# Value tiles of two strided attention groups: computed in token order and sorted by residue through DRAM

## Chip, cores, metric

One core of a Trainium2 chip runs the kernel. The metric is the device time of one launch in microseconds (us), the median of several runs. The engines are TensorE (PE in the profile; PEld is its weight load), VectorE (DVE), ScalarE (ACT), GpSimd (POOL) and SyncE (SP), which issues DMAs.

## What is computed

One layer of a decoder trunk: 512 tokens, width 1024, float32. One projection gives queries, keys and values of three token mixers and three gates; their outputs are gated, merged, projected and normalised, and a squared-ReLU MLP follows. The change touches the third mixer, a dilated window attention with three groups of four heads of 128 columns:

```python
DIL_PAIRS = ((128, 1), (512, 4), (2048, 16))   # window, dilation of group 0, 1, 2

def dilated_group(q, k, v, bias_table, window, dilation):
    # Query t reads t, t-d, ..., t-window.
    def to_strided(a):
        a = jnp.pad(a, ((0, 0), (0, Lp * dilation - S), (0, 0), (0, 0)))
        a = a.reshape(B, Lp, dilation, H, dh).transpose(0, 2, 3, 1, 4)
        return a.reshape(B, dilation, H, nb, n, dh)
    ...
    o = jnp.einsum('brhcqk,brhckd->brhcqd', prob.astype(vb.dtype), vb)
```

In groups 1 and 2 a query reads only keys of its own residue (token number modulo 4, or modulo 16). The kernel keeps both groups sorted by residue modulo 4: tile c holds the 128 tokens c, c+4, c+8, ...

## The kernel before

Every matmul operand is split into a high and a low part of the type that TensorE reads in one pass (`xh`, `xl` for the input, `h`, `l` for weights), and a product is three matmuls: high by high, high by low, low by high.

The work is a list of items. An item of kind "T" computes 128 columns of the projection, transposed (`mm3`, L87 to L89); kind "V" computes values, 128 tokens by 512 columns in each of four items (`v_items`, L331 to L333). An item of 24 matmuls goes into one of two PSUM banks and is copied out by ACT or DVE in turn (`cp`, L96 and L98; for values the copy makes the tile `V[name, g, tt]`). Weights come by SP's queue (`raw`, L182), and ACT and DVE split them (`wh`, L212; `wl`, L214) into a ring of seven chunks.

The main loop walks the items in the order of `main_order` and calls `step()` once before each item and once in its middle. A step resumes the attention generators that are active (`sb_head`, `dil_head`, `da_block`) and those in `pending`; what they issue falls between matmuls of the items. So the list of items and the number of steps set the order on each engine.

`dil_head` computes the scores of one head for the three groups, normalises them (L1540, L1544), transposes them on TensorE (L1556 for group 0, L1565 for groups 1 and 2), steps on until all values are there, and multiplies them by the value tiles (L1577 for group 0, L1582 for 1 and 2), with `po[:, c::4]` putting the columns of residue c back in token order. The wait for the values is a test while the program is written, not on the chip:

```python
while any(("dl_v", g, 3) not in V for g in range(3)):
    yield
po = at_bank()
```

The values of group g stand in the list after the second head's queries and keys of that group. For g > 0 their items read the input with a stride of four tokens (`xh[k][:, tt::4]`) as the stationary operand, so each tile comes out holding one residue.

POOL's queue carries sums of weight tiles for later stages: `gsum`, `usum`, `dsum`, copied from DRAM to DRAM (L804) and accumulated (L802) in pieces of 512 KB. Each is tied to a weight split on DVE, which spreads them over the main stream. POOL issues its DMAs in program order. The attention tiles live in 42 buffers of one pool (`slot`); a tile takes over a buffer when the last user of the tile before has finished.

Of the kernel before, what the change touches and what calls it, by code (L numbers as in the profile page):

```python
# [10 lines left out]
F32 = mybir.dt.float32  # L11
# [5 lines left out]
S = 512  # L17
D = 1024
P = 128
# [36 lines left out]
def trunk(tc, a, out):  # L56
    nc = tc.nc
    es = ExitStack()
    with es:
# [4 lines left out]
        dram = es.enter_context(tc.tile_pool(name="dram", bufs=1, space=bass.MemoryType.DRAM))  # L64
# [5 lines left out]
        def nm(s):  # L70
            uid[0] += 1
            return f"{s}_{uid[0]}"

        def slot(name, dt=F32):
            return big.tile([P, 512], dt, name=nm(name), tag="s", bufs=NSLOT)
# [7 lines left out]
        def at_bank():  # L83
            return psum.tile([P, 512], F32, name=nm("at"), tag="at", bufs=6)
# [8 lines left out]
        def cp(o, i):  # L93
            flip[0] ^= 1
            if flip[0]:
                nc.scalar.copy(o, i)  # L96
            else:
                nc.vector.tensor_copy(o, i)  # L98
# [53 lines left out]
        def chunk(src, w):  # L152
            return chunk_of(load(src, w))
# [78 lines left out]
        def item(cs, mm, ev, need=None, bank=None, size=1.0):  # L232
            items.append({"c": cs, "mm": mm, "ev": ev, "need": need, "bank": bank, "size": size})
# [9 lines left out]
        xh = [xhT[:, k, :] for k in range(8)]  # L243
        xl = [xlT[:, k, :] for k in range(8)]
# [7 lines left out]
        V = {}  # L252
# [42 lines left out]
        def first_item():  # L295
# [21 lines left out]
                    t_evac(*order[t][1:])(ps[t])  # L317
            item([cs[k][0] for k in (0, 1, 3, 5, 7)], mm, ev, bank=lambda: (at_bank(), at_bank()))

        def v_items(nv, name, g):  # L320
            cs = [chunk(a["wv"][nv, c].rearrange("p k n -> p (k n)"), 1024) for c in range(4)]
            for tt in range(4):
                def mm(ps, tt=tt):
                    for k in range(8):
                        c = cs[k // 2]
                        s = slice((k % 2) * 512, (k % 2) * 512 + 512)
                        if name == "dl_v" and g > 0:
                            x1, x2 = xh[k][:, tt::4], xl[k][:, tt::4]
                        else:
                            x1, x2 = xh[k][:, tt * P:tt * P + P], xl[k][:, tt * P:tt * P + P]  # L330
                        nc.tensor.matmul(ps, x1, c["h"][:, s], start=k == 0, stop=False)  # L331
                        nc.tensor.matmul(ps, x1, c["l"][:, s], start=False, stop=False)  # L332
                        nc.tensor.matmul(ps, x2, c["h"][:, s], start=False, stop=k == 7)  # L333
                        if k == 3:
                            yield

                def ev(ps, tt=tt):
                    if name == "sb_v":
                        v = [slot(name, F32R).rearrange("p (h two d) -> p h two d", two=2, d=64) for _ in range(2)]
                        pv = ps.rearrange("p (h d) -> p h d", d=64)  # L340
                        for i in range(2):
                            hs = slice(4 * i, 4 * i + 4)
                            nc.scalar.copy(v[i][:, :, 0, :], pv[:, hs, :])
                            nc.vector.tensor_sub(v[i][:, :, 1, :], pv[:, hs, :], v[i][:, :, 0, :].bitcast(F32))
                        V[name, g, tt] = v
                    else:
                        t = slot(name)
                        cp(t, ps)
                        V[name, g, tt] = t
                item(cs if tt == 3 else [], mm, ev, need=cs)  # L350

        nt, nv = 2, 0
# [2 lines left out]
        for kind, name, j in order[2:]:  # L355
            if kind == "T":
                if name == "gate":
                    continue
                t_item(nt, name, j)
                nt += 1  # L360
            else:
                v_items(nv, name, j)
                nv += 1
# [200 lines left out]
        x1 = {}  # L564
# [1026 lines left out]
        pending = []  # L1591
# [232 lines left out]
```

## Time and profile before

| | us |
|---|---|
| median of 3 runs (1065.19 to 1065.71) | 1065.29 |
| the profiled execution, own time | 1065.43 |
| its span, first to last instruction | 1063.7 |
| TensorE busy | 1051.9 |
| VectorE busy | 750.8 |
| ScalarE busy | 558.5 |
| GpSimd busy | 129.6 |

The profile is of one execution. The groups of its page name an instruction by line, engine, operation, and tiles as out<-in. Matmuls overlap, so the start of one to the start of the next, not the duration, is what one costs. The values of group 0 are computed between 142 and 169 us, of group 1 between 185 and 213, of group 2 between 226 and 259; the first two heads' products with the values lie between 266 and 274.

### The profile page before, as it was taken

The numbers are of one execution on the slowest core, as the hardware profiler recorded it, in microseconds if no ns is written. First come the engines' busy times: TensorE is split into PE (matmuls) and PEld (weight loads), VectorE is DVE, ScalarE is ACT, GpSimd is POOL, SyncE is SP. The second block draws the span as 40 slices with busy tenths as digits, with TensorE's granted clock in tenths as the row PEclk, the third lists the DMA queues.
The fourth block names the chain that finished last, engine by engine and source line by source line (L and its number), as shares of the span: only waits on it lengthen the run. The fifth ranks groups of instructions, "written<-read, shape, count | busy, mean of one in ns | idle before, by whom it ended". The sixth has DMA issues, their size and how long they took to land.

```text
span 1063.7 us, 15533 instructions
## 1 busy us (share of the span) xinstructions
PE 1051.9 (99%) x5826; PEld 913.4 (86%) x5826; DVE 750.8 (71%) x1345; ACT 558.5 (53%) x975; POOL 129.6 (12%) x200
## 2 busy tenths in 40 slices
PE   9999999999999999999999999999999999999996
PEld 6887788999888888888999988888999989989885
DVE  6888667547353757768767774888677877877965
ACT  7665545425232546447545452685765665665741
POOL 0000402021121102230111030101100010000000
PEclk9999999999999999999999999999999999999999
DMA  8333756393896819783766583149989788867602
GB/s 316 131 130 100 222 135 175 122 304 84 285 242 200 230 40 315 146 251 98 195 185 191 185 285 139 61 145 273 264 279 275 241 238 258 256 226 245 187 17 79
DMA packets 59452, 206.11 MB, mean 194 GB/s; under 512 B 7433, under 2 KB 8345, under 8 KB 59377
## 3 DMA queue, kind: packets, MB, share of 16 engines
q1 hardware_dynamic: 36192, 123.66, 33.4%
q0 software_dynamic: 22608, 80.55, 29.4%
q8 instruction: 45, 0.74, 0.3%
q10 hardware_dynamic: 576, 0.92, 0.2%
q14 instruction: 31, 0.25, 0.1%
HBM read 202.97 MB, written 73.42 MB: 260 GB/s over the span
## 4 chain that ended last, share of the span: by engine, by line
PE 89%; DVE 7%; issue 2%; ACT 2%; DMA 0%; POOL 0%; SPq 0%; DVEq 0%; POOLq 0%
PE mm L87 13%; PE mm L89 13%; PE mm L88 13%; PE at L87 4%; PE at L962 4%; PE at L963 4%; PE at L964 4%; PE at L89 4%; PE at L88 4%; PE mm L331 3%; PE mm L333 3%; PE mm L332 3%; DVE wl L214 2%; PE at L131 1%; PE at L312 1%
## 5 line engine op out<-in xcount | busy, mean ns | idle before, releaser
L212 ACT CAST wh<-raw 128x1024 fp32r<-128x1024 f32 (+1 forms) x243 | 250.7, 1035 | 254.6 <-PE mm L88 149.5
L214 DVE TENSOR_TENSOR wl<-raw,wh 128x1024 fp32r<-128x1024 f32 (+1 forms) x243 | 291.6, 1205 | 110.4 <-ACT wh L212 106.9
L87 PE MATMUL mm<-xhT,wh 128*128 128x512 f32 x368 | 146.8, 399 | 0.0
L89 PE MATMUL mm<-xhT,wl 128*128 128x512 f32 x368 | 144.5, 393 | 0.0
L88 PE MATMUL mm<-xlT,wh 128*128 128x512 f32 x368 | 144.1, 392 | 0.0
L89 PEld LDWEIGHTS mm<-xhT,wl 128*128 128x128 f32 x368 | 69.1, 188 | 15.0 <-DVE wl L214 0.3
L87 PEld LDWEIGHTS mm<-xhT,wh 128*128 128x128 f32 x368 | 69.2, 188 | 13.7 <-issue 0.4
L88 PEld LDWEIGHTS mm<-xlT,wh 128*128 128x128 f32 x368 | 69.2, 188 | 13.0
L962 PE MATMUL at<-wh,hh 128*128 128x512 f32 x188 | 73.7, 392 | 0.0
L963 PE MATMUL at<-wl,hh 128*128 128x512 f32 x188 | 73.7, 392 | 0.0
L87 PE MATMUL mm<-x1hT,wh 128*128 128x256 f32 x256 | 73.7, 288 | 0.0
L964 PE MATMUL at<-wh,hl 128*128 128x512 f32 x188 | 73.1, 389 | 0.0
L88 PE MATMUL mm<-x1lT,wh 128*128 128x256 f32 x256 | 72.3, 283 | 0.0
L89 PE MATMUL mm<-x1hT,wl 128*128 128x256 f32 x256 | 71.9, 283 | 0.0
L331 PE MATMUL mm<-wh,xhT 128*128 128x512 f32 x160 | 64.6, 404 | 0.0
L333 PE MATMUL mm<-wh,xlT 128*128 128x512 f32 x160 | 63.1, 394 | 0.0
L332 PE MATMUL mm<-wl,xhT 128*128 128x512 f32 x160 | 62.9, 393 | 0.0
L802 POOL DMA_DIRECT2D usum<-in_wu_dram x32 | 27.6, 862 | 233.5 <-DVE wl L214 222.0
L87 PEld LDWEIGHTS mm<-x1hT,wh 128*128 128x128 f32 x256 | 48.8, 191 | 4.7 <-ACT up L896 2.7
L88 PEld LDWEIGHTS mm<-x1lT,wh 128*128 128x128 f32 x256 | 48.9, 191 | 1.5
L89 PEld LDWEIGHTS mm<-x1hT,wl 128*128 128x128 f32 x256 | 48.6, 191 | 0.0
L802 POOL DMA_DIRECT2D dsum<-in_wd_dram x28 | 26.2, 935 | 133.5 <-DVE wl L214 128.5
(435 smaller groups left out, 2560.5 us busy)
## 6 DMA issues: line engine op xcount, KB each, us to landing
usum<-in_wu_dram POOLq DMA_DIRECT2D x48, 512.0 KB, 7.9
raw<-in_wt_dram SPq DMA_DIRECT2D x46, 512.0 KB, 5.1
dsum<-in_wd_dram POOLq DMA_DIRECT2D x42, 512.0 KB, 9.0
raw<-usum SPq DMA_DIRECT2D x32, 512.0 KB, 5.7
raw<-dsum SPq DMA_DIRECT2D x28, 512.0 KB, 5.0
raw<-in_wd_dram SPq DMA_DIRECT2D x25, 512.0 KB, 4.7
raw<-in_wu_dram SPq DMA_DIRECT2D x24, 512.0 KB, 6.6
raw<-in_wv_dram SPq DMA_DIRECT2D x20, 512.0 KB, 5.6
```

Of the source, the lines that this page charges most:

```text
L87: nc.tensor.matmul(ps, wh, xh, start=start, stop=False, skip_group_check=True)
L88: nc.tensor.matmul(ps, wh, xl, start=False, stop=False, skip_group_check=True)
L89: nc.tensor.matmul(ps, wl, xh, start=False, stop=stop, skip_group_check=True)
L212: i = nc.scalar.copy(h, raw)
L214: i = nc.vector.tensor_sub(lo, raw, h.bitcast(F32))
L331: nc.tensor.matmul(ps, x1, c["h"][:, s], start=k == 0, stop=False)
L332: nc.tensor.matmul(ps, x1, c["l"][:, s], start=False, stop=False)
L333: nc.tensor.matmul(ps, x2, c["h"][:, s], start=False, stop=k == 7)
L802: i = nc.gpsimd.dma_start(o, i, accum_op=OP.add, max_dma_last_dim=4096)
L962: nc.tensor.matmul(ps, h[:, q], c["h"][:, s], start=go, stop=False, skip_group_check=True)
L963: nc.tensor.matmul(ps, h[:, q], c["l"][:, s], start=False, stop=False, skip_group_check=True)
L964: nc.tensor.matmul(ps, lo[:, q], c["h"][:, s], start=False, stop=end, skip_group_check=True)
```

## The change

The values of groups 1 and 2 are computed like those of group 0, from 128 consecutive tokens. Each of the four tiles is stored to a DRAM tensor `vd[g]` after its copy from PSUM. A generator in `pending` passes two steps after the last store, issues four loads, each of every fourth row of `vd[g]`, passes three more steps, and only then enters the loaded tiles as `V["dl_v", g, c]`. Stores and loads are issued by POOL.

```diff
+        vd = {g: dram.tile([S, 512], F32, name=f"vd{g}") for g in (1, 2)}
+
+        def by_residue(g):
+            for _ in range(WRITE):
+                yield
+            ts = []
+            for c in range(4):
+                t = slot("dl_v")
+                nc.gpsimd.dma_start(t, vd[g].rearrange("(n c) d -> c n d", c=4)[c])
+                ts.append(t)
+            for _ in range(READ):
+                yield
+            for c in range(4):
+                V["dl_v", g, c] = ts[c]
+
+        WRITE, READ = 2, 3
+
         def v_items(nv, name, g):
...
-                        if name == "dl_v" and g > 0:
-                            x1, x2 = xh[k][:, tt::4], xl[k][:, tt::4]
-                        else:
-                            x1, x2 = xh[k][:, tt * P:tt * P + P], xl[k][:, tt * P:tt * P + P]
+                        x1, x2 = xh[k][:, tt * P:tt * P + P], xl[k][:, tt * P:tt * P + P]
                         nc.tensor.matmul(ps, x1, c["h"][:, s], start=k == 0, stop=False)
...
                         t = slot(name)
                         cp(t, ps)
-                        V[name, g, tt] = t
+                        if name == "dl_v" and g > 0:
+                            nc.gpsimd.dma_start(vd[g][tt * P:tt * P + P, :], t)
+                            if tt == 3:
+                                pending.append(by_residue(g))
+                        else:
+                            V[name, g, tt] = t
```

## The prediction

> **What bounds the kernel now.** I read the page first: span, busy times, the chain that ended last.
>
> ```profile
> span 1063.7 us, 15533 instructions
> PE 1051.9 (99%) x5826; PEld 913.4 (86%) x5826; DVE 750.8 (71%) x1345; ACT 558.5 (53%) x975; POOL 129.6 (12%) x200
> PE 89%; DVE 7%; issue 2%; ACT 2%; DMA 0%; POOL 0%; SPq 0%; DVEq 0%; POOLq 0%
> ```
>
> TensorE is busy 99% of the span and 89% of the last chain. A microsecond that its stream of matmuls loses or saves anywhere in the middle goes almost whole into the time; DMA and POOL matter only when TensorE has to wait for them.
>
> Next, the view of one source line, L331, whole and then between 184 and 213 us, where group 1 is computed. The figures after the colon are ns, least/median/most.
>
> ```profile
> L331 PEld LDWEIGHTS mm<-wh,xhT x160: 187/188/333, 32.6 to 401.5; 128*128 128x128 f32 x160
> ...
> L331 PEld LDWEIGHTS mm<-wh,xhT x32: 308/310/317, 184.7 to 212.1; 128*128 128x128 f32 x32
> ```
>
> The weight load of a token slice with stride 4 takes 310 ns, the usual one 188. Whether that reaches the matmuls is told by the timeline of TensorE (start, duration in us).
>
> ```profile
> 142.35 0.40 PE L331 MATMUL mm<-wh,xhT 128*128 128x512 f32 x1
> ...
> 151.03 0.40 PE L331 MATMUL mm<-wh,xhT 128*128 128x512 f32 x1
> ...
> 156.29 0.39 PE L333 MATMUL mm<-wh,xlT 128*128 128x512 f32 x1
> ...
> 184.92 0.40 PE L331 MATMUL mm<-wh,xhT 128*128 128x512 f32 x1
> ...
> 190.33 0.39 PE L333 MATMUL mm<-wh,xlT 128*128 128x512 f32 x1
> ...
> 191.27 0.51 PE L331 MATMUL mm<-wh,xhT 128*128 128x512 f32 x1
> ...
> 255.19 0.60 PE L331 MATMUL mm<-wh,xhT 128*128 128x512 f32 x1
> ...
> 274.03 0.47 PE L87 MATMUL mm<-xhT,wh 128*128 128x512 f32 x1
> 274.35 0.40 PE L88 MATMUL mm<-xlT,wh 128*128 128x512 f32 x1
> ...
> 284.36 0.39 PE L87 MATMUL mm<-xhT,wh 128*128 128x512 f32 x1
> ```
>
> **The gain.** 151.03 to 156.29 is one item of group 0 (24 matmuls, 23 steps): 0.2287 us a step. 184.92 to 190.33 is one of group 1: 0.2352. So most of the longer load lies under the matmul before it, and 0.0065 comes through (0.0077 against the 44 steps from 274.35 to 284.36, 0.2275 each). It comes through more where TensorE returns from attention work with short matmuls: the first matmul takes 0.51 instead of 0.40 (191.27 against 142.35, after 256-column matmuls) and 0.60 instead of 0.47 (255.19 against 274.03, after fp32 ones). The two groups have 2 x 4 x 24 = 192 such matmuls. I count ten such returns in the timeline, the first and one of the last of them shown: four of 0.11 to 0.12, one of 0.06, five of 0.125, together about 1.15 us. The other 182 give 182 x 0.0065 to 0.008 = 1.2 to 1.5. Sum: 2.35 to 2.65; I take **2.45 us**, 1.1 of it in group 1 and 1.35 in group 2.
>
> A rule speaks against this: the Trainium skill, "TensorE: Matmul & The Clock Gate", section "LDWEIGHTS (loading the stationary operand)", has the load's time depend on the number of columns alone, about 107 ns for 128, with no word of stride, and its section "Step-by-step: what each phase is for" has it run under the matmul before. By it the gain would be nothing. The trace disagrees: 310 against 188 ns, and 0.2352 against 0.2287 between matmuls.
>
> **What is added.** Per group: four stores of 256 KB (each behind its copy from PSUM) and four loads of 256 KB, all issued by POOL, on the queue of the weight sums. The order of the built program shows the rest: nothing moves on TensorE but the value products of heads 0 and 1 (L1577, L1582). They go from their place after the transposes to a point one and nearly two items later, since the five steps of the generator pass first. ACT and DVE keep their order, but for copies of those products.
>
> ```profile
> 266.63 1.68 PE L1577 MATMUL at<-pt,dl_v 128*128 128x256 f32 x8
> 268.15 1.95 PE L1582 MATMUL at<-pt,dl_v 128*128 128x128 f32 x16
> 269.94 1.04 PE L1565 MATMUL at<-ident,L 128*128 128x128 f32 x8
> 270.81 1.68 PE L1577 MATMUL at<-pt,dl_v 128*128 128x256 f32 x8
> ...
> 266.22 1.13 DVE L1544 TENSOR_SCALAR L<-L,mxx 128x256 f32<-128x256 f32 x4
> ```
>
> The two blocks take 269.94 - 266.63 = 3.31 and 274.03 - 270.81 = 3.22 us; they now stand before the matmul that starts at 284.36. Moving them uncovers the transposes L1565: they come straight after L1556, at 266.63 on the old clock, and need the four scalings L1544, done one after another from 266.22 to 267.35. The third block of columns cannot be transposed before about 267.1, the fourth before 267.35: **+0.4 us**, where the first products hid it before. The blocks now stand alone, one more change between fp32 and the rounded kind (0.32 against 0.23 us to the next matmul): **+0.1**.
>
> **Do the loads arrive in time?** TensorE comes to the products at 284.36 - 6.53 - 2.45 + 0.4 = 275.8. The products with group 0 take 268.15 - 266.63 = 1.52, those with group 1 half of 269.94 - 268.15, 0.9; so the first tile of group 2 is wanted at 278.2 and the fourth, three products of 0.22 later, at 278.8. What stands in POOL's queue then (timeline; below each stretch of it the issues of narrow windows, in the same order, with the us from issue to landing):
>
> ```profile
> 258.03 0.81 POOL L802 DMA_DIRECT2D usum<-in_wu_dram  x1 [23.46 <-DVE wl L214]
> 258.56 1.13 POOL L802 DMA_DIRECT2D dsum<-in_wd_dram  x1
> ...
> 258.79 0.69 DVE L98 COPY dl_v<-mm 128x512 f32<-128x512 f32 x1
> ...
> 262.87 0.52 POOL L804 DMA_DIRECT2D dsum<-in_wd_dram  x1 [0.92 <-DVE sel L1522]
> 269.24 0.52 POOL L804 DMA_DIRECT2D usum<-in_wu_dram  x1 [5.86 <-DVE wl L214]
> 269.75 0.52 POOL L804 DMA_DIRECT2D dsum<-in_wd_dram  x1
> usum<-in_wu_dram POOLq DMA_DIRECT2D x1, 512.0 KB, 6.4
> dsum<-in_wd_dram POOLq DMA_DIRECT2D x1, 512.0 KB, 10.5
> dsum<-in_wd_dram POOLq DMA_DIRECT2D x1, 512.0 KB, 14.5
> usum<-in_wu_dram POOLq DMA_DIRECT2D x1, 512.0 KB, 9.4
> dsum<-in_wd_dram POOLq DMA_DIRECT2D x1, 512.0 KB, 10.1
> ...
> 298.38 2.48 POOL L1187 DMA_DIRECT2D sh<-rv  x4
> sh<-rv POOLq DMA_DIRECT2D x4, 256.0 KB, 9.1
> out_dram<-xn ACTq DMA_DIRECT2D x1, 256.0 KB, 2.0
> ```
>
> The last store of group 2 follows the copy that ends at 259.48, so it is queued behind the two accumulating sums (landed 264.4 and 269.1). Four plain copies of 512 KB follow, the last landing at 262.87 + 14.5 = 277.4. The loads wait for the store, are issued near 268, and stand behind those copies. With the gain the stage is 2.45 earlier: 274.9. Then five pieces of 256 KB are extra, the store and four loads. A piece costs half of what the sums show, 269.1 - 264.4 = 4.7 for 512 KB, so 2.3, as the upper bound; the lower bound is 0, for a store that fits into a gap (alone, one takes 2.0 us from issue to landing, the last row). The two plain copies issued last land at 278.6 and 279.9, 1.2 apart, so 0.6 for 256 KB. The nearest rows in kind are the four table loads of 256 KB, issued in 2.48 us and landing 9.1 (median) after issue, so in queue one behind the other; they bracket nothing tighter. I take 1.0, nearer to the plain copies than to the sums: the fourth load lands at 279.9 and TensorE waits **1.1 us** (0 to 7.6 by the bounds; 274.9 + 5 x 2.3 = 286.4). Everything on TensorE queues behind this wait.
>
> By the Trainium skill, "DMA: Bandwidth & Descriptors", section "Anatomy of one DMA — SWDGE (gpsimd) path", a transfer takes 2.0 us plus its bytes at 436 GB/s, an estimate of 2.6 us for 256 KB; store and loads would be over near 265, and the sum would be the one without this wait. The 14.5 us of the row at 262.87 disagree, because the queue is not empty.
>
> Group 1 has the same hop 40 us before its use; that cover is ample. Its last store has another reader, though: the tile's buffer goes to a later attention tile, so DVE's L1366 now waits for the store's landing.
>
> ```profile
> 213.61 0.96 POOL L802 DMA_DIRECT2D usum<-in_wu_dram  x1
> usum<-in_wu_dram POOLq DMA_DIRECT2D x1, 512.0 KB, 11.9
> ...
> 223.30 0.36 DVE L1366 CAST ah<-a 128x384 fp32r<-128x384 f32 x1 [1.75 <-ACT a L1363]
> ...
> 224.77 0.69 DVE L1367 TENSOR_TENSOR al<-a,ah 128x512 fp32r<-128x512 f32 x1
> ...
> 229.91 0.28 PE L1378 MATMUL at<-al,sb_v 128*64 128x256 f32 x1
> ```
>
> The sum ahead lands at 225.5, the store 0.6 to 2.3 later, both 1.1 earlier in the new run: 225.0 to 226.7. L1366 would have started at 222.2, so DVE stands 2.8 to 4.5 us, with the split, a key copy and a weight split queued behind. The cover is 229.91 - (224.77 + 0.69) = 4.45 us until TensorE reads the result. **0** in the sum; 0.1 at the bound, and whatever the store lands later than 226.7 goes one for one to TensorE. The weight splits behind it feed a ring seven deep. The weight sums that POOL issues a few us later are read in later stages. The view of the waits has POOL standing 222 us for the weight splits that pace them:
>
> ```profile
> POOL usum L802 <- DVE wl L214: 222.0, 25, 36.0
> ```
>
> So a sum that is late by a few us has idle time to catch up in: 0, and SP's loads of the sums would pay if it hadn't.
>
> **Sum.** The profiled execution took 1065.43 us (span 1063.7 and 1.7 around it; the median of the runs is 1065.29). 1065.43 - 2.45 + 0.4 + 0.1 + 1.1 + 0 = **1064.6 us**. A measurement of this kernel can tell about 0.2%, 2.1 us, from no change, so this is a saving inside that bound.
>
> **Rivals.**
> Everything covered: the extra pieces cost 0.6 or less, the fourth load lands by 277.9 and nothing waits. The time is then 1063.5, and 1062.8 if the gain is 2.65 and the transposes do not wait. For it: the 0.6 of the two plain copies. Against: it needs every term at its good end. It passes the 0.2% bound only with both of the last conditions.
>
> Late loads (slower): the mechanism above at the price of the accumulating sums. One load is 2.3 us, the fourth lands at 286.4, TensorE waits 7.6: 1071.1. Past 1.6 us a piece (fourth load at 282.9, a wait of 4.1) the change is slower by over 0.2%. For it: every DMA of this stretch is 6 to 15 us from issue to landing, and the loads need the store first. Against: the pieces are plain ones.
>
> A buffer wait on DVE or ACT: the last store of group 1 lands 4 us later than I work out, near 230. DVE then stands over 7 us and TensorE 4: 1068.6. Against it: a sum of 512 KB is 4.7 us behind the one before, and the store has half its bytes.
>
> No gain: the load is hidden and the change only adds: 1064.6 + 2.45 = 1067.0. The steps of 0.2352 speak against it.
>
> **How the numbers follow.** Forecast (1063.8 to 1067): 0.44. Everything covered: 0.25, of it 0.17 past the bound. Late loads (1067 to 1071): 0.2, of it 0.18 past the bound. DVE: 0.07, nearly all past it. No gain: 0.04, half past it. Faster by over 0.2%: 0.17; slower: 0.18 + 0.07 + 0.02 = 0.27; within: 0.56. The range is 1062.8, the good end of every term, to 1068.5, which leaves the far half of the late loads and part of the DVE case out. The likeliest case's own range is 1063.8 to 1067.
>
> **What would show it.** Right: weight loads of L331's successor all near 188 ns; steps of 0.228 in groups 1 and 2; a wait of 0.5 to 2 us on TensorE before the products with group 2, ended by a load; 0.4 before the transposes. Wrong: no idle time there (covered), more than 4 us there (late loads), idle time near 228 ended by DVE (buffer wait), steps still at 0.235 (no gain).

## The result, and the profile after

The changed kernel takes **1070.72 us** (median of 8 runs, 1067.46 to 1074.38), the kernel before on the same chip 1065.6 (1065.19 to 1066.04): a ratio of 1.0047, 95% interval 1.0035 to 1.006. It is slower by 5 us, and where the runs of before lie within 1 us, those of after lie within 7. The profiled execution is one of the shortest: own time 1067.54, 2.1 over that of before.

The page of after first: span, busy times, the chain that ended last.

```profile
span 1065.8 us, 15575 instructions
PE 1051.2 (99%) x5826; PEld 903.9 (85%) x5826; DVE 750.7 (70%) x1345; ACT 558.5 (52%) x975; POOL 138.5 (13%) x216
PE 83%; DVE 8%; DMA 3%; issue 3%; ACT 2%; POOL 1%; SPq 0%; DVEq 0%; POOLq 0%
```

TensorE is busy 0.7 us less in a span that is 2.1 longer, and DMA, which had no share of the last chain, has 3%. The view of the value line (L346, before L331) and two rows of TensorE's timeline show that the gain itself came:

```profile
L346 PEld LDWEIGHTS mm<-wh,xhT x160: 187/188/200, 32.8 to 402.5; 128*128 128x128 f32 x160
...
185.09 0.39 PE L346 MATMUL mm<-wh,xhT 128*128 128x512 f32 x1
...
190.30 0.40 PE L348 MATMUL mm<-wh,xlT 128*128 128x512 f32 x1
```

No weight load takes 310 ns any more, and an item of group 1 has steps of (190.30 - 185.09) / 23 = 0.2265 us instead of 0.2352. Matched matmul by matmul against before, TensorE gains 1.1 us in group 1 (from 0.2 behind at 184 us to 0.9 ahead at 213) and 1.0 in group 2 (between 229 and 262). The rest is loss. The first loss is near 228, behind the first matmuls of group 2, in the timelines of DVE and TensorE:

```profile
219.40 1.22 DVE L214 TENSOR_TENSOR wl<-raw,wh 128x1024 fp32r<-128x1024 f32 x1 [1.80 <-ACT wh L212]
226.66 0.36 DVE L1386 CAST ah<-a 128x384 fp32r<-128x384 f32 x1 [6.03 <-DMA vd<-dl_v]
...
228.12 0.69 DVE L1387 TENSOR_TENSOR al<-a,ah 128x512 fp32r<-128x512 f32 x1
...
228.87 0.44 PE L1398 MATMUL at<-al,sb_v 128*64 128x512 f32 x1 [0.30 <-DVE al L1387]
```

DVE stands 6.03 us until the last store of group 1 has landed and so freed the buffer. The matmul that reads DVE's last result has 0.30 of idle time before it; by the starts of the matmuls, TensorE loses 0.6 in all here. The second loss is larger: the value products of the first two heads.

```profile
276.62 1.68 PE L1597 MATMUL at<-pt,dl_v 128*128 128x256 f32 x8
278.13 1.48 PE L1602 MATMUL at<-pt,dl_v 128*128 128x128 f32 x10
280.55 0.97 PE L1602 MATMUL at<-pt,dl_v 128*128 128x128 f32 x4 [0.94 <-DMA dl_v<-vd]
281.70 0.49 PE L1602 MATMUL at<-pt,dl_v 128*128 128x128 f32 x2 [0.18 <-DMA dl_v<-vd]
282.03 1.68 PE L1597 MATMUL at<-pt,dl_v 128*128 128x256 f32 x8
283.55 1.95 PE L1602 MATMUL at<-pt,dl_v 128*128 128x128 f32 x16
285.25 0.47 PE L87 MATMUL mm<-xhT,wh 128*128 128x512 f32 x1
```

Undisturbed, the four groups take 6.52 us (the last experiments show it); here 285.25 - 276.62 = 8.63, so 2.1 is lost, and the rows name the loads as what ended the waits. After that, two small things: a wait of 0.34 at 541, and 0.8 at the end of the program, which comes back below.

Two views tell how the DMAs stood: issues with the time to landing, and windows of 5 us. A row of the second has the window, its length, the busy time of PE, PEld, DVE, ACT and POOL (in brackets the number of instructions), the granted clock (1.00 is full speed), the DMA engines' busy share, and the GB/s that they moved.

```profile
dl_v<-vd POOLq DMA_DIRECT2D x4, 256.0 KB, 9.5
vd<-dl_v POOLq DMA_DIRECT2D x1, 256.0 KB, 10.9
...
265.00:270.00 5.00, 5.00 (x29) 4.11 (x28) 3.34 (x8) 1.68 (x3) 0.00 (x0) 1.00 1.01 339
270.00:275.00 5.00, 5.00 (x23) 4.14 (x23) 1.92 (x2) 1.06 (x1) 2.75 (x6) 1.00 1.03 419
275.00:280.00 5.00, 4.62 (x26) 3.83 (x24) 1.23 (x1) 1.54 (x2) 1.91 (x4) 1.00 1.02 378
280.00:285.00 5.00, 4.27 (x27) 3.74 (x28) 0.00 (x0) 0.58 (x1) 0.44 (x1) 1.00 1.03 420
```

From 260 to 285 us the busy share of the 16 DMA engines is 1.01 or more in every window. In before, the same view falls from 275 on:

```profile
275.00:280.00 5.00, 5.00 (x23) 4.12 (x23) 0.71 (x2) 1.06 (x1) 0.00 (x0) 1.00 0.69 282
280.00:285.00 5.00, 5.00 (x23) 4.14 (x23) 1.20 (x1) 0.62 (x1) 1.02 (x2) 1.00 0.53 186
```

So the five added pieces go where the engines were just getting free.

### The profile page after: what moved, and what is told of

Read it like the earlier page. It is cut to its first block, busy times and chain, and to the rows that moved or that the text cites. A ratio compares the mean times of both kernels' runs of the same rounds, so it can differ in the third digit from the quotient of the medians.

```text
span 1065.8 us, 15575 instructions
## 1 busy us (share of the span) xinstructions
PE 1051.2 (99%) x5826; PEld 903.9 (85%) x5826; DVE 750.7 (70%) x1345; ACT 558.5 (52%) x975; POOL 138.5 (13%) x216
## 4 chain that ended last, share of the span: by engine, by line
PE 83%; DVE 8%; DMA 3%; issue 3%; ACT 2%; POOL 1%; SPq 0%; DVEq 0%; POOLq 0%
PE mm L87 12%; PE mm L89 12%; PE mm L88 12%; PE at L87 4%; PE at L982 4%; PE at L983 4%; PE at L984 4%; PE at L89 4%; PE at L88 4%; PE mm L346 3%; PE mm L348 3%; PE mm L347 3%; DVE wl L214 2%; DMA vd<-dl_v 2%; PE at L131 1%
## 5 line engine op out<-in xcount | busy, mean ns | idle before, releaser
L87 PE MATMUL mm<-xhT,wh 128*128 128x512 f32 x368 | 146.9, 399 | 0.0
L87 PEld LDWEIGHTS mm<-xhT,wh 128*128 128x128 f32 x368 | 69.2, 188 | 13.7 <-issue 0.4
L87 PE MATMUL mm<-x1hT,wh 128*128 128x256 f32 x256 | 73.6, 288 | 0.0
L346 PE MATMUL mm<-wh,xhT 128*128 128x512 f32 x160 | 63.3, 396 | 0.0
L87 PEld LDWEIGHTS mm<-x1hT,wh 128*128 128x128 f32 x256 | 48.8, 190 | 4.7 <-ACT up L916 2.7
```

The costliest lines, as they stand in the source:

```text
L87: nc.tensor.matmul(ps, wh, xh, start=start, stop=False, skip_group_check=True)
```

## Experiments

Each is a small edit of the changed kernel; times are medians. The kernel before, on the same chip in each batch, took 1065.4 to 1065.7.

| kernel | us | runs from, to | ratio to before, 95% |
|---|---|---|---|
| again | 1069.37 | 1067.39, 1071.55 | 1.0025 to 1.0052 |
| gain_only | 1063.37 | 1062.94, 1063.60 | 0.9972 to 0.9989 |
| hop_only | 1070.32 | 1068.02, 1071.92 | 1.0029 to 1.0054 |
| read6 | 1065.21 | 1064.77, 1066.90 | 0.9990 to 1.0007 |
| act_all | 1072.84 | 1071.44, 1073.81 | 1.0052 to 1.0080 |
| act_store | 1067.06 | 1066.22, 1068.16 | 1.0006 to 1.0023 |
| act_load | 1076.90 | 1076.78, 1078.23 | 1.0096 to 1.0124 |
| hold | 1073.31 | 1070.41, 1073.60 | 1.0053 to 1.0078 |
| act_store6 | 1064.00 | 1063.58, 1064.82 | 0.9979 to 0.9997 |
| hold_out | 1065.64 | 1065.01, 1068.67 | 0.9996 to 1.0014 |
| hold_act | 1064.16 | 1063.43, 1064.30 | 0.9978 to 0.9996 |
| again2 | 1069.23 | 1067.89, 1072.35 | 1.0033 to 1.0056 |

### Gain and price apart

**again**: the changed kernel, unaltered.

> The changed kernel unaltered, for a second profile and more times. Theory A (the loads of group 2 come late, by an amount that changes from run to run, and a store of group 1 holds DVE): 1067 to 1074 us, and the profiled execution's time above 1065.4 is explained by TensorE's idle time before the products with group 2 (0.5 to 8 us) and near 228 us (0 to 2 us), less a gain of 2.0 to 2.4 us. Theory B (a pause makes the clock drop, and that is what costs): the profile shows a stretch at half clock in the middle of the span, not only after the last matmul. Theory C (4 MB more of DMA make later stages wait): the loss builds up after 300 us.

**gain_only**: contiguous slices, no stores, no loads.

```diff
-                        if name == "dl_v" and g > 0:
-                            nc.gpsimd.dma_start(vd[g][tt * P:tt * P + P, :], t)
-                            if tt == 3:
-                                pending.append(by_residue(g))
-                        else:
-                            V[name, g, tt] = t
+                        V[name, g, tt] = t
```

> Values in token order, without stores and loads; the tiles are used as they are, so the order by residue is left out. All theories: the gain by itself. Steps of 0.228 us in groups 1 and 2, and 1063.1 to 1063.7 us (2.0 to 2.4 below before), with runs within 0.5 us of each other. If the weight load's stride is worth nothing: 1065.5.

**hop_only**: the way through DRAM (the hop), with the slices of stride 4 kept.

```diff
-                        x1, x2 = xh[k][:, tt * P:tt * P + P], xl[k][:, tt * P:tt * P + P]
+                        if name == "dl_v" and g > 0:
+                            x1, x2 = xh[k][:, tt::4], xl[k][:, tt::4]
+                        else:
+                            x1, x2 = xh[k][:, tt * P:tt * P + P], xl[k][:, tt * P:tt * P + P]
...
-                nc.gpsimd.dma_start(t, vd[g].rearrange("(n c) d -> c n d", c=4)[c])
+                nc.gpsimd.dma_start(t, vd[g][c * P:c * P + P, :])
```

> The stride-4 matmuls of before, and the stores, loads and steps of the change (the loads read 128 rows in a row). Theory A: the cost by itself, 3 to 9 us over before (1068 to 1074), runs as wide apart as the changed kernel's, idle time before the products with group 2. Theory C: the same total, but most of it after 300 us. If the hop cost only what the first profile of the change shows, 1068.3.

**read6**: the products 36 matmuls later.

```diff
-        WRITE, READ = 2, 3
+        WRITE, READ = 2, 6
```

> The changed kernel with READ = 6 instead of 3: the products with the values of heads 0 and 1 stand 36 matmuls (8.2 us) later, nothing else moves. Theory A: the late loads are covered, only DVE's wait near 228 us is left (0.3 to 1 us on TensorE): 1063.5 to 1065, with runs within 1 us of each other. Theory B: as theory A, for want of a pause. Theory C: 1067 to 1073 as before, since the traffic is the same.

The contiguous slices alone bring 1065.45 - 1063.37 = 2.1 us; the hop alone costs 1070.32 - 1065.45 = 4.9. The profile of again has no half clock before the end of the program, and TensorE loses only 0.4 us after 300, so it shows nothing of theories B and C. Giving the loads 8 us more takes away most of the price: 1065.21. So most of the loss is the wait for group 2's loads. What read6 still lacks against gain_only, 1.8 us, is DVE's wait near 228 (0.57 in its trace), the 0.8 at the end of the program, 0.2 to 0.3 for the moved products, and a rest. Its expectation was missed in part: the median lies 0.2 above the 1063.5 to 1065 of theory A, and the runs are 2.1 us apart, not 1.

### Queue or bandwidth

The loads stood behind POOL's weight sums. My first reading was POOL's queue, and the next four runs were to show it. The edits put `nc.scalar` for `nc.gpsimd`: in **act_all** at the stores and the loads, in **act_store** at the stores alone, in **act_load** at the loads alone. **hold** keeps both on POOL and was to hold back the sums (`credit` counts the sums that POOL may issue next). The edits of act_all, then of hold:

```diff
-                nc.gpsimd.dma_start(t, vd[g].rearrange("(n c) d -> c n d", c=4)[c])
+                nc.scalar.dma_start(t, vd[g].rearrange("(n c) d -> c n d", c=4)[c])
...
-                            nc.gpsimd.dma_start(vd[g][tt * P:tt * P + P, :], t)
+                            nc.scalar.dma_start(vd[g][tt * P:tt * P + P, :], t)
```

```diff
                 ts.append(t)
+            hold[0] = 0
...
+        hold = [0]
...
+                        if name == "dl_v" and g == 2 and tt == 2:
+                            hold[0] = 1
...
-            while credit >= 1:
+            while credit >= 1 and not hold[0]:
```

> All eight stores and eight loads are issued by ACT, on its own queue; their places in the program and all else stay (TensorE's order is the same). Queue theory (a store lands 11 us after its issue because two accumulating sums stand ahead of it in POOL's queue, a load 9 us after because of four plain copies): stores land 2 to 4 us after issue, the loads of group 2 before 275 us, nothing waits before the products with group 2, and DVE's wait near 228 is gone too. Time 1063.5 to 1064.7 (1063.4 of the kernel that has the contiguous slices alone, 0.2 for the moved products, 0 to 0.8 at the end). Hop theory (the way through DRAM is slow by itself, or by the weight loads that share the 16 DMA engines): the loads still land after 278, the time stays above 1066.5 and varies by several us from run to run.

> Only the eight stores are issued by ACT; the loads stay on POOL. Queue theory: the last store of group 2 lands near 263 instead of 270, POOL issues the loads near 264, but behind the four plain copies, so they land between 272 and 278: TensorE waits 0 to 1 us, DVE's wait near 228 is gone. Time 1063.6 to 1065.5. Hop theory: as with everything on ACT's queue, above 1066.5.

> Only the eight loads are issued by ACT; the stores stay on POOL. Queue theory: the last store of group 2 lands near 270 as before, ACT stands 2 to 3 us for it, the loads land 2 to 5 us after, by 275; no wait of TensorE for them or one under 0.5 us; the wait for DVE near 228 stays (0.65). Time 1064.3 to 1066. If the loads themselves are the slow part (reading rows 8 KB apart), they still land 9 us after issue, and the time is above 1066.5.

> The hop stays on POOL's queue; the weight sums are held back from the third value item of group 2 until its loads are issued, and caught up afterwards. Queue theory: the stores of group 2 land within 3 us, the loads by 272; no wait before the products. The wait for DVE near 228 (0.65) and 0.8 at the end stay: 1064.4 to 1065.8, unless the sums that come later are missed by a later stage. Hop theory: no change, 1067.5 to 1072.

The queue theory fell: all four are slower than it allows. Away from the sums' queue, the loads of group 2 take longer to land, not less. Issues of act_all, act_load, act_store and hold in the stretch from 255 to 290, one row each:

```profile
dl_v<-vd ACTq DMA_DIRECT2D x4, 256.0 KB, 11.5
```

```profile
dl_v<-vd ACTq DMA_DIRECT2D x4, 256.0 KB, 11.0
```

```profile
dl_v<-vd POOLq DMA_DIRECT2D x4, 256.0 KB, 10.4
```

```profile
dl_v<-vd POOLq DMA_DIRECT2D x4, 256.0 KB, 17.3
```

Why, TensorE's timeline of act_all shows:

```profile
278.19 1.68 PE L1597 MATMUL at<-pt,dl_v 128*128 128x256 f32 x8
279.70 1.74 PE L1602 MATMUL at<-pt,dl_v 128*128 128x128 f32 x12
283.80 0.49 PE L1602 MATMUL at<-pt,dl_v 128*128 128x128 f32 x2 [2.35 <-DMA dl_v<-vd]
286.72 0.80 PE L1602 MATMUL at<-pt,dl_v 128*128 128x128 f32 x2 [2.44 <-DMA dl_v<-vd]
287.31 3.19 PE L1597 MATMUL at<-pt,dl_v 128*128 128x256 f32 x8
290.29 2.57 PE L1602 MATMUL at<-pt,dl_v 128*128 128x128 f32 x16
292.62 0.48 PE L87 MATMUL mm<-xhT,wh 128*128 128x512 f32 x1
```

The four loads land at 278.3, 280.9, 283.8 and 286.7: the first no later than on POOL, each next one 2.6 to 2.9 us after, where on POOL's queue it was 0.5 to 1.4 (279.1, 280.5, 281.0, 281.7). The engines are full (418 GB/s at a share of 1.03 from 280 to 285, as in after); a second queue gets a share of them instead of a turn, and the sums of POOL's queue now run beside the loads: one issued at 262.16 lands at 280.1, between the first two. This reading is called the bandwidth theory below. It is what the Trainium skill says in "DMA: Bandwidth & Descriptors", section "Issuing engines are not separate DMA queues": DMAs of the different issuing engines end up on the same 16 engines and interleave. No run issues the loads from ACT while the sums are out of the way, so for loads a slowness of ACT's own queue is not excluded.

The times of act_all and act_load hold a second price, which is no evidence on queue or bandwidth. ACT issues the loads of group 1 in its program order, and each must wait for the store, so ACT itself stands until the last store of group 1 has landed (timeline of ACT in act_all):

```profile
227.68 0.98 ACT L1383 ACTIVATE a<-at 128x384 f32<-128x384 f32 x2 [7.90 <-issue]
```

In act_load it is 8.43. DVE and TensorE wait for what ACT makes next: TensorE loses 2.2 us near 228 in act_all and 2.7 in act_load, and act_load has half clock behind it.

With act_store the loads keep POOL's queue, and DVE's wait near 228 costs TensorE nothing: 1067.06. Its last store of group 2 lands at 267.7 from ACT's queue, 10.4 after issue, where the queue theory had 263. hold did not do what it was meant to: the built program has five sums, four of them accumulating, between the last store and the loads, and the loads take 17.3 us; it says what sums in front cost, not what their absence brings.

### The sums out of the way

**hold_out** holds the sums from the second item of group 2 until the generator has passed READ and two more steps; in the built program POOL then issues stores, loads, sums, and the order on the other engines is that of the change. **hold_act** has the stores on ACT's queue as well. **act_store6** is act_store with READ = 6. The edit of hold_out, where `hold = [0]` and the loop are as in hold:

```diff
             for c in range(4):
                 V["dl_v", g, c] = ts[c]
+            for _ in range(2):
+                yield
+            hold[0] = 0
...
+                        if name == "dl_v" and g == 2 and tt == 1:
+                            hold[0] = 1
```

> The hop as in the change (READ = 3, all on POOL), but the weight sums that POOL would issue between the second value item of group 2 and the loads are issued after the loads; the order on TensorE, ACT and DVE is unchanged. Bandwidth theory: with 4 MB of sums out of the way the last store lands near 263, the loads by 270, and TensorE does not wait for them: 1063.4 + 0.65 (DVE near 228, group 1) + 0.15 + 0.8 (end) = 1064.8 to 1065.8, and the granted clock stays at 1.0 until the end. If the way through DRAM is slow by itself, the loads still land near 280 and the time stays at 1067.5 to 1074.

> The same with the stores on ACT's queue (the sums behind the loads, READ = 3). Bandwidth theory: no wait of TensorE at either place, 1063.4 + 0.15 + 0.4 = 1063.8 to 1064.4. If sums that are 10 us later are missed by a later stage, 1065 or more, with a new wait after 290 us.

> Stores issued by ACT, loads by POOL, READ = 6 in place of 3, so the products with group 2 stand 36 matmuls later. Bandwidth theory (the 16 DMA engines move about 420 GB/s without a break from 260 to 285 us, and the five extra pieces end wherever that stream ends, whatever queue they stand in): the loads land near 281 as with the stores alone on ACT, are wanted at 286, nothing waits; DVE's wait near 228 is gone as it was there. Time 1063.4 (contiguous slices alone) + 0.15 (moved products) + 0.4 (end of the program, half of the 16 DMAs on POOL) = 1063.8 to 1064.4, a spread of the runs under 1.5. If instead a further cost of the traffic itself exists, it stays at 1065 or above.

The medians of all three lie where the bandwidth theory had them. Two of the 11 runs of hold_out took 1068.7, 3 us more than expected; its profile is not of one of them, and their cause stays open. Issues and windows of hold_out:

```profile
dl_v<-vd POOLq DMA_DIRECT2D x4, 256.0 KB, 3.6
vd<-dl_v POOLq DMA_DIRECT2D x1, 256.0 KB, 5.0
...
260.00:265.00 5.00, 5.00 (x27) 4.07 (x25) 4.50 (x18) 1.72 (x3) 0.42 (x1) 1.00 0.90 338
265.00:270.00 5.00, 5.00 (x29) 4.10 (x27) 3.32 (x7) 1.67 (x3) 3.03 (x7) 1.00 0.83 249
```

Same hop, same queue, same products: with the sums behind them the loads take 3.6 us instead of 9.5, the fourth lands at 269.9 instead of 281.7, and no matmul waits for it. So the way through DRAM is not slow by itself. Between queue and bandwidth hold_out does not decide, since it takes the sums out of both; act_store and hold_act do. In both the last store of group 2 stands on ACT's queue and the sums on POOL's: it lands 10.4 us after issue with the sums beside it, 4.9 without them. What is left of hold_out's price is DVE's wait (0.8 in its trace), the moved products (0.2), the end (0.8) and a wait of 0.34 at 541. hold_act loses none of the first, and its products show the undisturbed length, 282.33 - 275.81 = 6.52:

```profile
275.81 1.68 PE L1603 MATMUL at<-pt,dl_v 128*128 128x256 f32 x8
277.32 1.95 PE L1608 MATMUL at<-pt,dl_v 128*128 128x128 f32 x16
279.11 1.68 PE L1603 MATMUL at<-pt,dl_v 128*128 128x256 f32 x8
280.63 1.95 PE L1608 MATMUL at<-pt,dl_v 128*128 128x128 f32 x16
282.33 0.48 PE L87 MATMUL mm<-xhT,wh 128*128 128x512 f32 x1
```

Its last matmul ends at 1053.77, gain_only's at 1053.74, after a start that was 0.3 earlier: the hop costs TensorE those 0.3 of the moved products then, and no more. hold_act and act_store6 beat both kernels, by 0.0003 to 0.0022 of the time of before (both intervals together): 1.3 and 1.4 us by the medians, less than the 0.2% named in the prediction, but with intervals that exclude 1. act_store6 needs no change to the sums.

### Why the runs differ

**again2**: the changed kernel once more.

> The changed kernel once more, unaltered, for the granted clock. Its runs lie between 1067.4 and 1074.4 with mean clocks of 0.998 to 0.994. If the later ones are those in which the wait for group 2's loads makes the clock drop: a profile at or above 1070 shows a stretch of half clock of 3.4 us or a multiple of it right behind that wait, one below 1069 none.

The profiled execution took 1067.89 and shows half clock only at the end, as expected of one below 1069; none of the three profiles of the changed kernel fell above 1069, so the other half of the expectation stayed untested there. Other kernels of the study show half clock behind the waits. In act_store the clock falls behind the waits (windows of TensorE alone; the third figure from the right is the granted clock):

```profile
277.00:280.00 3.00, 1.89 (x13) 1.00 1.02 415
280.00:282.00 2.00, 1.86 (x7) 0.67 1.03 422
282.00:284.00 2.00, 2.00 (x8) 0.50 1.03 420
```

```profile
278.29 0.49 PE L1602 MATMUL at<-pt,dl_v 128*128 128x128 f32 x2 [0.48 <-DMA dl_v<-vd]
279.25 0.49 PE L1602 MATMUL at<-pt,dl_v 128*128 128x128 f32 x2 [0.47 <-DMA dl_v<-vd]
...
281.01 3.20 PE L1597 MATMUL at<-pt,dl_v 128*128 128x256 f32 x8
```

The eight matmuls of L1597 take 3.20 instead of 1.68. The stretch of half clock lasts 3.41 us there, 6.83 in act_all and hold, and 3.41 and 10.24 in act_load, each time right behind waits that the hop brings. But waits do not always do it: the profile of again waits twice as long at this place, 2.48 us in all, at full clock (windows of TensorE alone):

```profile
277.00:280.00 3.00, 1.96 (x15) 1.00 1.04 367
280.00:283.00 3.00, 1.56 (x9) 1.00 1.01 411
```

A stretch of 3.41 us lowers the mean clock of a run by 3.41 x 0.5 / 1067 = 0.0016. Of the 19 runs of the changed kernel, those up to 1069.4 us have means of 0.997 or 0.998 with one exception (1069.29 with 0.996), and of the ten above, eight have 0.994 to 0.996. So about half of the runs seem to pay for the late loads twice, in waiting and in half clock. For the changed kernel this rests on the means alone, and the half clock at the end of the program, 5.2 to 8.8 us in the profiles, moves a mean by up to 0.0016 as well; no profile caught it in the act.

## Why the prediction was wrong

The forecast was 1064.6, inside the bound; the result is slower by 0.47% and past the range (1062.8 to 1068.5). Its rival "late loads" is what happened in kind. That its 1071.1 lies near the median is luck: it has 2.3 us for each piece, and the loads cost 1.06 each. By its own steps, in the profiled execution:

- **The gain, 2.45**: 2.1 measured (gain_only). Group 1 has its 1.1. Group 2 brought 1.1 instead of 1.35: in gain_only two of the five returns after fp32 matmuls still take 0.425 to the next start (0.434 before), and the 0.125 counted for each was never theirs. Right in kind, a term too large.
- **The transposes, 0.4, and the switch, 0.1**: 0.2 to 0.3 together: so much do read6, hold_out and hold_act fall behind gain_only on TensorE from 229 us to behind the products. About twice too large.
- **DVE's wait, 0**: 0.6. The store landed at 226.56, within the 225.0 to 226.7 forecast, though the sum ahead of it landed only 0.25 earlier than in before (225.23 against 225.48), not 1.1. The failed step is the cover. It was measured to the matmul at 229.91, which reads another tile; the first reader of the last split in before is this one:

```profile
229.22 0.39 PE L1378 MATMUL at<-al,sb_v 128*64 128x512 f32 x1
```

That leaves 229.22 - 225.46 = 3.8 instead of 4.45, and the gain of 1.0 by then brings the reader that much nearer, which the step left out: 2.8 of cover. DVE's split started 3.36 later than before (226.66 against 223.30), so 0.6 goes to TensorE.
- **The loads, 1.1**: 2.1 in the profiled execution, 2.45 in that of again2, 3.55 in that of again; the other executions have no profile, and most of them took longer. The price of a piece was right: the four loads landed 4.2 us behind the queue, 1.06 each, against 1.0. The failed step is "with the gain the stage is 2.45 earlier". The first sum of that stretch is issued at 257.21 against 258.03, only 0.8 earlier, because group 2's share of the gain was not in yet and 0.6 had gone to DVE; the store put the sum behind it back by 1.4 instead of 1.0; so the queue ended at 277.4, as in before, not at 275.9. The fourth load landed at 281.7 instead of 279.9.
- **The end, not in the sum**: 0.8.
- **The clock, not in the sum**: the prediction took the time of one profiled execution for that of all. With a wait that depends on when a full DMA queue drains, 1 us of shift is 1 us of wait, and in some runs the clock seems to add its own, 1.7 us for each stretch of 3.41 at half clock. That would make the difference between 1067.54, which the range held, and the median of 1070.72; with no profile of a run above 1069, how it divides between waiting and clock stays open.

Sum of the profiled execution: 1065.43 - 2.1 + 0.6 + 0.2 + 2.1 + 0.34 + 0.8 = 1067.4, against 1067.54. The wait of 0.34 at 541 (L87, for a result of DVE's L547) stands in the profiles of again, again2, hop_only, act_store and hold_out too, and not in read6, act_store6 or hold_act; nothing run here explains it.

The estimate by the Trainium skill ("DMA: Bandwidth & Descriptors", section "Anatomy of one DMA — SWDGE (gpsimd) path"), 2.6 us for 256 KB, was set aside for the rows of a full queue, and that was right for the change, where the loads took 9.5. With the sums out of the way they took 3.6 (hold_out), an issue of 0.5 each among it.

## What to carry over

A transfer that was put into a stretch where the DMA engines were full was not priced by its bytes but by when the stream ahead of it ended, and another issuing engine's queue did not get past that stream, it only shared it: move the other traffic or the reader. An engine that issues a load of what was just stored stands until the store has landed, so count what that engine had to do meanwhile. Read a cover to the first instruction that needs the result, and subtract from it what the change itself gains by then. A wait of TensorE at a busy place is a term with a spread, so compare several runs before trusting one profile of it.

## What was not expected of the hardware

**Half clock after short waits.** In act_store no single wait on TensorE was over 0.49 us (1.26 us in all within 2.7 us), and the clock was halved for 3.41 us. The Trainium skill, "TensorE: Matmul & The Clock Gate", section "Part 1: The HAM clock gate", has a window of 3413 ns, which the stretches of 3.41, 6.83 and 10.24 us fit; the full idle window that it asks for before the clock falls was not there. Idle time alone does not decide either: again had 2.48 us of it within 4 us, in waits of up to 1.15, and kept full clock. What decides is not shown here.

**POOL's DMAs cost time at the end of the program.** From the issue of the last output rows to the end of the span (timeline and span of before, after and hold_act):

```profile
1059.22 1.12 SPq L1112 DMA_DIRECT2D out_dram<-xn  x2
```

```profile
1060.52 1.12 SPq L1132 DMA_DIRECT2D out_dram<-xn  x2
```

```profile
1057.36 1.12 SPq L1138 DMA_DIRECT2D out_dram<-xn  x2
span 1062.3 us, 15570 instructions
```

Before has 1063.7 - 1059.22 = 4.5 us, after 1065.8 - 1060.52 = 5.3, hold_act with 8 of the 16 DMAs on POOL 4.9, and act_all with none 4.5: 0.05 us for each DMA that POOL issues, in POOL's closing instruction (5.7 us in before, 6.5 in read6).
